# Key norms folded into the new values, token-side key scaling on ScalarE, and products of a head pair grouped by shape

## The chip, the cores and the metric

The kernel runs on one core of one Trainium2 chip. The metric is the device time of one execution in microseconds (us). Five engines work side by side, each with its own in-order instruction stream: TensorE (PE, its weight loads PEld), VectorE (DVE), ScalarE (ACT), GpSimd (POOL) and the queue that issues transfers (SP).

## The reference, cut to what matters

Two blocks follow each other on one sequence of 512 tokens with model width 1024. The first mixes a gated delta rule of 8 heads with causal attention of 8 heads and ends in a gated feed-forward; the second holds a state-space mixer (SSD) of 16 heads and a short convolution. What the change touches:

```
# gated delta rule, chunks of c tokens (the kernel: 4 chunks of 128), one head
k = l2norm(k);  q = l2norm(q) * dk**-0.5
decay = tril(exp(g_i - g_j))
lmat  = (beta*k) k^T * decay                       # the kernel's ln, with sign
sol   = solve(I + strict_lower(lmat), [beta*v, beta*k*exp(g)])
v_new = u - w @ state                              # the kernel's gvn
o     = (q*exp(g)) @ state + (q k^T * decay) @ v_new   # q k^T * decay: at
state = state*exp(g_last) + (k*exp(g_last - g))^T @ v_new   # k*exp(..): ktok

# state-space mixer, chunks of 128 tokens, heads in pairs m = 0..7
y_diag = (C B^T * decay_in) @ xd
y_off  = (C * decay_out) @ previous_state
y      = y_diag + y_off
```

## The kernel before, in words

The sequence lies along the free dimension: a tile is 128 features by 512 tokens. All weights come as one stream of 512 KB chunks (eight blocks of 128x128). ScalarE rounds a chunk into `hi`, VectorE or GpSimd makes the rest `lo`, and `linear` multiplies each block three times (hi by hi, hi by lo, lo by hi), so one linear of eight blocks is 24 products of 512 columns. These land in PSUM tiles called `mm`; all smaller products and transposes land in tiles called `pt`, of which there are four.

The order of the linears in the first block is written out by hand in `GDN_ORDER`: `kq` (key and query of a head), `vg` (value and gate), `brb` and `bra` (gates of the two branches), `low` (not a linear: it starts the norms of the attention's low-rank inputs, `cq` and `ckv`), `att` (a head of attention), `wv` (the attention's values), `ya` (output product of the delta rule). The same list orders the weight stream. Around the linears run generator tasks. A planner (`Timeline`, `drive`) prices every instruction as it is emitted and always goes on with the task whose next step is ready first by its model; the main task with the linears comes last among equals. So the instruction order of every engine is fixed when the program is built, and comes from modelled times, not from the chip's.

A head of the delta rule has two tasks. `t_gdn_a` transposes key and query to token-major, takes their squared norms on ScalarE (`ss`), turns them into reciprocal roots `r` in twelve small VectorE steps (`rsqrt`), scales the token-major key into `ktok`, and makes the two 128x128-per-chunk matrices `ln` (key by key) and `at` (key by query). At most two such tasks are open. When four heads are through, `t_solve` inverts the 32x32 diagonal blocks for these four on VectorE and GpSimd, and `t_gdn_b` (at most three open) completes the inverse and runs the four chunks of the recurrence: `gr`, `gvn` (the new values), the state `gst`, and the output. `ya` waits for all eight heads.

In the second block `t_ssd` handles a pair of heads. For each chunk it issues two products of 128 rows by 64 columns (one for each head, in the two halves of the output's partitions) and, from the second chunk on, two of 64 by 64 that add the contribution of the state before. Each fp32 product shows as two records in the trace. The loop before the change reads:

```python
for c in range(NC):
    for e in range(2):
        self.MM(py[o(e), cc], self.xd[m][:, ...], Es[e][:, cc], start=True, stop=(c == 0))
    if c:
        for e in range(2):
            self.MM(py[o(e), cc], self.st[c - 1][r, hh(e)], Cs[e][r, cc], start=False, stop=True)
```

Of the kernel before, what the change touches and what calls it, by code (L numbers as in the profile page):

```python
# [12 lines left out]
AF = mybir.ActivationFunctionType  # L13
ALU = mybir.AluOpType
# [7 lines left out]
NC = 4  # L22
# [6 lines left out]

START = ["ab", ("cq", 0), ("cq", 1), ("cq", 2)]  # L30
FIRST = [("k", 0), ("q", 0), ("k", 1)]
GDN_ORDER = [("brb", 0), ("kq", 3), ("brb", 1), ("brb", 2), ("kq", 4), ("brb", 3), ("vg", 0), ("brb", 4), ("vg",
             1), ("vg", 2), ("kq", 5), ("kq", 6), ("kq", 7), ("vg", 3), ("vg", 4), ("brb", 5), ("brb", 6),
             ("brb", 7), ("vg", 5), ("vg", 6), ("low",), ("bra", 0), ("bra", 1), ("bra", 2), ("vg", 7), ("att",
             0), ("bra", 3), ("wv", 0), ("att", 1), ("bra", 4), ("bra", 5), ("bra", 6), ("bra", 7), ("ya", 0),
             ("att", 2), ("ya", 1), ("att", 3), ("wv", 1), ("ya", 2), ("att", 4), ("ya", 3), ("att", 5), ("ya",
             4), ("att", 6), ("att", 7), ("ya", 5), ("ya", 6), ("ya", 7)]
PAIR_FFN = 3
FOLD_FFN = 3
# [360 lines left out]
class Emit:  # L400
# [564 lines left out]
    def t_gdn_a(self, h, kq):  # L965
        nc = self.nc
        hs = slice(4 * h, 4 * h + 4)
        yield self.flag("gates")

        yield lambda: "k" in kq  # L970
        k = kq["k"]
        yield [k]
        ss = self.s(8, "ss")
        pk = self.transpose4(k)
        junk = self.g(name="junk")
        yield [pk]
        for c in range(NC):
            nc.scalar.activation(junk[:, self.cc(c)], pk[:, self.cc(c)], AF.Square, accum_out=ss[:, c:c + 1])
        yield lambda: "q" in kq
        q = kq["q"]  # L980
        yield [q]
        pq = self.transpose4(q)
        yield [pq]
        for c in range(NC):
            nc.scalar.activation(junk[:, self.cc(c)], pq[:, self.cc(c)], AF.Square, accum_out=ss[:, 4 + c:5 + c])
        yield [ss]
        nc.vector.tensor_scalar(ss, ss, EPS, None, ALU.add)
        r = yield from self.rsqrt(ss, 8, "rkq")
        col = self.s(8, "kcol")
        nc.vector.tensor_tensor(col[:, 0:4], self.kdec[:, hs], r[:, 0:4], ALU.mult)  # L990
        del junk
        kt = self.g(name="ktok")
        nc.vector.tensor_tensor(self.v4(kt), self.v4(pk), self.colbc(col[:, 0:4]), ALU.mult)
        nc.vector.tensor_copy(self.rq[:, hs], r[:, 4:8])
        nc.vector.tensor_tensor(self.nk[:, hs], ss[:, 0:4], r[:, 0:4], ALU.mult)
        nc.vector.tensor_tensor(self.bk[:, hs], self.cmp[:, 64 + 4 * h:68 + 4 * h], r[:, 0:4], ALU.mult)
        nc.vector.scalar_tensor_tensor(col[:, 4:8], self.bk[:, hs], -1.0, r[:, 0:4], ALU.mult, ALU.mult)
        yield lambda: h in self.E
        e = self.E.pop(h)
        egb = self.rowload(self.grow[1, h])  # L1000
        yield [e]
        at = self.g(name="at")
        ln = self.g(name="ln")
        for t, x, f in ((ln, k, col[:, 4:8]), (at, q, r[:, 0:4])):
            p = self.mm4(k, x)
            yield [p]
            for c in range(NC):
                nc.vector.scalar_tensor_tensor(t[:, self.cc(c)], p[:, self.cc(c)], f[:, c:c + 1], e[:, self.cc(c)],
                                               ALU.mult, ALU.mult)
        yield [ln]  # L1010
        for b in range(4):
            nc.sync.dma_start(
                self.ldram[h, :, b].rearrange("c j i -> j c i"),
                self.v4(ln)[32 * b:32 * b + 32, :, 32 * b:32 * b + 32])
        yield [egb]
        nc.gpsimd.tensor_tensor(q, q, egb, ALU.mult)
        self.hd[h] = dict(kd=kt, kT=k, ln=ln, at=at, qd=q)
        self.flags.add(("L", h))
        h0 = h - h % NSOLVE
        if all(("L", i) in self.flags for i in range(h0, h0 + NSOLVE)):  # L1020
            self.spawn(self.t_solve(h0, NSOLVE), "solve")
# [29 lines left out]
    def t_gdn_b(self, h, vg):  # L1051
        nc = self.nc
# [3 lines left out]
        hs = slice(4 * h, 4 * h + 4)  # L1056
# [5 lines left out]
        ln = d.pop("ln")  # L1062
# [12 lines left out]
        p = self.transpose4(v)  # L1075
# [14 lines left out]
        p = self.pt()  # L1090
# [37 lines left out]
        for c in range(NC):  # L1128
            cc = self.cc(c)
            col = slice(4 * h + c, 4 * h + c + 1)  # L1130
            if c == 0:
                r = vb[:, cc]
            else:
                yield [st]
                p = self.pt()
                self.MM(p[:, 0:128], d["kT"][:, cc], st, start=True, stop=True)
                r = self.s(128, "gr")
                yield [p]
                nc.vector.scalar_tensor_tensor(r, p[:, 0:128], self.neg_eg[:, col], vb[:, cc],
                                               ALU.mult, ALU.add)  # L1140
            yield [Y, r]
            p = self.pt()
            self.MM(p[:, 0:128], Y[:, cc], r, start=True, stop=True)
            vn = self.s(128, "gvn")
            yield [p]
            nc.vector.tensor_scalar(vn, p[:, 0:128], self.bk[:, col], None, ALU.mult)
            yield [vn]
            if c < NC - 1:
                p = self.pt()
                self.MM(p[:, 0:128], d["kd"][:, cc], vn, start=True, stop=True)  # L1150
                st2 = self.s(128, "gst", bufs=6)
                yield [p]
                if c == 0:
                    nc.vector.tensor_copy(st2, p[:, 0:128])
                else:
                    nc.vector.scalar_tensor_tensor(st2, st, self.glast[:, col], p[:, 0:128],
                                                   ALU.mult, ALU.add)
            p = self.pt()
            if c:
                self.MM(p[:, 0:128], d["qd"][:, cc], st, start=True, stop=False)  # L1160
            self.MM(p[:, 0:128], d["at"][:, cc], vn, start=(c == 0), stop=True)
            yield [p]
            nc.scalar.copy(on[:, cc], p[:, 0:128])
            nc.scalar.activation(junk[:, cc], p[:, 0:128], AF.Square, accum_out=so[:, c:c + 1])
            if c < NC - 1:
                st = st2
# [630 lines left out]
    def t_ssd(self, m, zd):  # L1797
        nc = self.nc
        g = m // 4
        r = slice(64 * g, 64 * g + 64)  # L1800
        yield self.flag("states")
        Es, Cs = [], []
        for h in (2 * m, 2 * m + 1):
            Es.append(self.rowload(self.crow[0, h]))
            Ce = self.g(name="Ce")
            nc.sync.dma_start(Ce[r], self.crow[1, h].partition_broadcast(64))
            Cs.append(Ce)
        for e in range(2):
            h, E = 2 * m + e, Es[e]
            yield [E]  # L1810
            for c in range(NC):
                nc.vector.tensor_scalar(E[:, self.cc(c)], E[:, self.cc(c)],
                                        self.cmp2[:, 4 * h + c:4 * h + c + 1], 0.0, ALU.subtract, ALU.min)
        for e in range(2):
            yield [Es[e]]
            nc.scalar.activation(Es[e], Es[e], AF.Exp)
        for e in range(2):
            yield [Es[e]]
            nc.vector.tensor_tensor(Es[e], Es[e], self.cb[g], ALU.mult)
            yield [Cs[e]]  # L1820
            nc.gpsimd.tensor_tensor(Cs[e][r], Cs[e][r], self.C[r], ALU.mult)
        yield Es + Cs + self.st
        py = self.pt()
        o = lambda e: slice(64 * e, 64 * e + 64)
        hh = lambda e: slice(64 * ((2 * m + e) % 8), 64 * ((2 * m + e) % 8) + 64)
        for c in range(NC):
            cc = self.cc(c)
            for e in range(2):
                self.MM(py[o(e), cc], self.xd[m][:, 128 * c + 64 * e:128 * c + 64 * e + 64], Es[e][:, cc],
                        start=True, stop=(c == 0))  # L1830
            if c:
                for e in range(2):
                    self.MM(py[o(e), cc], self.st[c - 1][r, hh(e)], Cs[e][r, cc], start=False, stop=True)
        y = self.xs[m]
        yield [py]
        nc.vector.scalar_tensor_tensor(y, y, self.par("d_skip_2", m), py, ALU.mult, ALU.add)
        yield lambda: m in zd
        yield [y, zd[m]]
        nc.gpsimd.tensor_tensor(y, y, zd[m], ALU.mult)
        self.yz[g][m % 4] = y  # L1840
# [215 lines left out]
```

## Time and profile before

| | |
|---|---|
| median of 3 runs | 1463.79 us (1463.4 to 1465.91) |
| the profiled execution | 1465.11 us, span 1463.3 us |
| mean granted clock of TensorE | 0.994 |
| busy: PE / PEld / DVE / ACT / POOL | 1443.4 / 1187.8 / 867.9 / 656.2 / 497.5 us |

The span runs from the first instruction to the last; the execution's time is 1.8 us longer than its span. Busy times are sums over the span. A matmul's end is modelled, so a TensorE that counts as busy may still lose time inside its records.

### The profile page before, as it was taken

The page shows a single profiled execution, that of the slowest core. Times are in us where ns is not written, and L with a number is a line of the kernel's source. Part 1 is how long each engine was busy: PE and PEld are TensorE (multiplying, and loading weights), DVE is VectorE, ACT ScalarE, POOL GpSimd, SP SyncE. Part 2 cuts the span into 40 slices and gives each one's busy share as a digit, 9 for nine tenths or more (in the row PEclk, how much of TensorE's full clock was granted, in tenths as well). Part 3 has the DMA queues.
Part 4 walks back from the last instruction along what each step waited for, and adds up shares of the span by engine and source line. Part 5 has one row for each costly group of instructions (what it writes and reads, how often), then busy time and mean ns, then how long its engine had stood idle before and what let it go on. Part 6 is the DMA issues. An engine that isn't in the chain of part 4 may idle for free.

```text
span 1463.3 us, 18957 instructions
## 1 busy us (share of the span) xinstructions
PE 1443.4 (99%) x7084; PEld 1187.8 (81%) x7084; DVE 867.9 (59%) x1722; ACT 656.2 (45%) x1120; POOL 497.5 (34%) x312
## 2 busy tenths in 40 slices
PE   9999999999999999999999999999999999999998
PEld 6788788878878888888888888888787788788877
DVE  7988879697755555368441144347764785351164
ACT  4665336244546664354442244444544454342252
POOL 0333500520333413403554455530215444534300
PEclk9999999999999999999999999999999999999999
DMA  5434313331132224433333333232224533323333
GB/s 191 133 117 140 113 58 86 108 109 32 52 93 65 80 72 132 149 94 101 101 101 96 92 101 101 86 101 87 88 87 108 149 104 115 115 87 95 97 96 101
DMA packets 56891, 147.62 MB, mean 101 GB/s; under 512 B 15008, under 2 KB 15584, under 8 KB 56800
## 3 DMA queue, kind: packets, MB, share of 16 engines
q1 hardware_dynamic: 56800, 146.42, 33.3%
q8 instruction: 55, 0.90, 0.2%
q14 instruction: 36, 0.29, 0.1%
HBM read 139.48 MB, written 5.34 MB: 99 GB/s over the span
## 4 chain that ended last, share of the span: by engine, by line
PE 81%; DVE 11%; POOL 3%; issue 2%; ACT 1%; DMA 1%; SPq 1%; DVEq 0%; POOLq 0%; ACTq 0%
PE mm L249 72%; PE pt L249 8%; DVE lo L249 2%; POOL st L249 1%; POOL sx L249 1%; DVE st L249 1%; SPq L249 1%; DVE row L249 1%; DVE sx L249 1%; ACT hi L249 0%; DVE Y L249 0%; DVE qrs L249 0%; DMA sl<-ldram 0%; DVE v L249 0%; DMA x<-xT 0%
## 5 line engine op out<-in xcount | busy, mean ns | idle before, releaser
L249 PE MATMUL mm<-hi,hi 128*128 128x512 f32 (+2 forms) x1872 | 740.4, 395 | 1.2 <-ACT hi L249 1.2
L249 PE MATMUL mm<-hi,lo 128*128 128x512 f32 (+2 forms) x1872 | 725.4, 388 | 2.4 <-DVE lo L249 2.4
L249 PE MATMUL mm<-lo,hi 128*128 128x512 f32 (+2 forms) x1872 | 725.9, 388 | 0.8 <-DVE lo L249 0.8
L249 POOL TENSOR_TENSOR lo<-raw,hi 128x1024 fp32r<-128x1024 f32 x136 | 327.6, 2409 | 462.2 <-ACT hi L249 399.6
L249 PEld LDWEIGHTS mm<-hi,lo 128*128 128x128 f32 x1872 | 352.0, 188 | 77.2 <-DVE lo L249 3.7
L249 PEld LDWEIGHTS mm<-hi,hi 128*128 128x128 f32 x1872 | 352.4, 188 | 71.1 <-ACT hi L249 2.1
L249 PEld LDWEIGHTS mm<-lo,hi 128*128 128x128 f32 x1872 | 352.7, 188 | 67.0 <-DVE lo L249 1.5
L249 ACT ACTIVATE hi<-raw 128x1024 fp32r<-128x1024 f32 (+1 forms) x230 | 242.4, 1054 | 226.5 <-PE mm L249 168.0
L249 DVE TENSOR_TENSOR lo<-raw,hi 128x1024 fp32r<-128x1024 f32 (+1 forms) x94 | 117.1, 1245 | 27.9 <-ACT hi L249 27.9
L249 DVE TENSOR_TENSOR sq<-sq,sq 128x512 f32<-128x512 f32 x43 | 31.9, 754 | 87.9 <-ACT sq L249 87.7
L249 DVE TENSOR_TENSOR xr<-xr,mm 128x512 f32<-128x512 f32 x24 | 16.5, 687 | 86.8 <-PE mm L249 86.8
L249 DVE TENSOR_TENSOR lo<-fu,hi 128x512 fp32r<-128x512 f32 x22 | 43.1, 1960 | 40.9 <-ACT hi L249 40.9
L249 DVE SCALAR_TENSOR_TENSOR fu<-mm,params,fu 128x510 f32<-128x510 f32 (+1 forms) x38 | 28.5, 749 | 65.3 <-ACT fu L249 64.6
L249 ACT ACT_TABLE_LOAD x39 | 50.0, 1283 | 15.5 <-DVE k L249 6.0
L249 POOL TENSOR_TENSOR fu<-fg,fu 128x512 f32<-128x512 f32 x22 | 30.2, 1373 | 65.6 <-DVE fu L249 35.2
L249 POOL TENSOR_TENSOR q<-q,row 128x512 f32<-128x512 f32 x8 | 10.5, 1318 | 96.6 <-PE pt L249 86.8
L249 POOL TENSOR_TENSOR st<-sl,sx 64x247 f32<-64x247 f32 (+15 forms) x31 | 20.8, 672 | 34.3 <-DVE sx L249 25.0
L249 DVE SCALAR_TENSOR_TENSOR fg<-mm,params,fg 128x510 f32<-128x510 f32 (+1 forms) x38 | 28.2, 743 | 6.2 <-ACT fg L249 5.5
L249 DVE TENSOR_TENSOR lo<-scz,hi 128x512 fp32r<-128x512 f32 x8 | 16.2, 2020 | 26.3 <-ACT hi L249 26.3
L249 DVE TENSOR_TENSOR lo<-pt,hi 128x512 fp32r<-128x512 f32 (+3 forms) x32 | 15.6, 488 | 26.2 <-ACT hi L249 26.0
L249 ACT ACTIVATE fg<-fg 128x512 f32<-128x512 f32 x22 | 13.9, 630 | 37.0 <-DVE fg L249 37.0
L249 DVE SCALAR_TENSOR_TENSOR xbc<-mm,params,xbc 128x509 f32<-128x509 f32 (+2 forms) x30 | 22.5, 749 | 9.5 <-ACT xbc L249 8.8
(311 smaller groups left out, 1531.6 us busy)
## 6 DMA issues: line engine op xcount, KB each, us to landing
raw<-wstream SPq DMA_DIRECT2D x228, 512.0 KB, 3.6
row<-grow_d SPq DMA_DIRECT2D x16, 256.0 KB, 4.4
row<-crow_d SPq DMA_DIRECT2D x16, 256.0 KB, 5.0
x<-xT SPq DMA_DIRECT2D x8, 256.0 KB, 6.0
sbd<-gate SPq DMA_DIRECT2D x8, 256.0 KB, 2.1
sb<-sbd SPq DMA_DIRECT2D x8, 256.0 KB, 3.8
xr<-xT SPq DMA_DIRECT2D x8, 256.0 KB, 3.7
Ce<-crow_d SPq DMA_DIRECT2D x16, 128.0 KB, 5.3
```

What stands on the lines that cost most here:

```text
L249: return f(*args, **kw)
```

## The change

In the delta rule the reciprocal key norm `r` no longer enters `ktok`, `at` and the new values once each; it enters the new values alone, as its square. `ktok` is scaled by the decay factor only, which is known before the norms, by four ScalarE copies right behind the key's squares; `at` is one VectorE product for all four chunks in place of four. The small column tiles change with it. In `t_ssd` all eight 128x64 products of a pair are issued first and then all six 64x64 products, with the accumulation flags to match. `GDN_ORDER` is a new list.

```diff
-GDN_ORDER = [("brb", 0), ("kq", 3), ("brb", 1), ("brb", 2), ("kq", 4), ("brb", 3), ("vg", 0), ("brb", 4), ("vg",
-             1), ("vg", 2), ("kq", 5), ("kq", 6), ("kq", 7), ("vg", 3), ("vg", 4), ("brb", 5), ("brb", 6),
-             ("brb", 7), ("vg", 5), ("vg", 6), ("low",), ("bra", 0), ("bra", 1), ("bra", 2), ("vg", 7), ("att",
-             0), ("bra", 3), ("wv", 0), ("att", 1), ("bra", 4), ("bra", 5), ("bra", 6), ("bra", 7), ("ya", 0),
-             ("att", 2), ("ya", 1), ("att", 3), ("wv", 1), ("ya", 2), ("att", 4), ("ya", 3), ("att", 5), ("ya",
+GDN_ORDER = [("kq", 3), ("brb", 0), ("brb", 1), ("brb", 2), ("kq", 4), ("vg", 0), ("brb", 3), ("brb", 4), ("vg",
+             1), ("vg", 2), ("kq", 5), ("kq", 6), ("kq", 7), ("vg", 3), ("vg", 4), ("brb", 5), ("vg", 5), ("brb",
+             6), ("brb", 7), ("bra", 0), ("bra", 1), ("vg", 6), ("low",), ("bra", 2), ("vg", 7), ("bra", 3),
+             ("att", 0), ("bra", 4), ("bra", 5), ("wv", 0), ("att", 1), ("bra", 6), ("bra", 7), ("ya", 0),
+             ("att", 2), ("ya", 1), ("att", 3), ("ya", 2), ("att", 4), ("wv", 1), ("att", 5), ("ya", 3), ("ya",
              4), ("att", 6), ("att", 7), ("ya", 5), ("ya", 6), ("ya", 7)]
@@ t_gdn_a, behind the squares of the key
+        kt = self.g(name="ktok")
+        for c in range(NC):
+            nc.scalar.activation(kt[:, self.cc(c)], pk[:, self.cc(c)], AF.Copy,
+                                 scale=self.kdec[:, 4 * h + c:4 * h + c + 1])
+        del pk
@@ t_gdn_a, behind the reciprocal roots
-        col = self.s(8, "kcol")
-        nc.vector.tensor_tensor(col[:, 0:4], self.kdec[:, hs], r[:, 0:4], ALU.mult)
+        col = self.s(4, "kcol")
-        kt = self.g(name="ktok")
-        nc.vector.tensor_tensor(self.v4(kt), self.v4(pk), self.colbc(col[:, 0:4]), ALU.mult)
-        nc.vector.tensor_tensor(self.bk[:, hs], self.cmp[:, 64 + 4 * h:68 + 4 * h], r[:, 0:4], ALU.mult)
-        nc.vector.scalar_tensor_tensor(col[:, 4:8], self.bk[:, hs], -1.0, r[:, 0:4], ALU.mult, ALU.mult)
+        nc.vector.tensor_tensor(col, self.cmp[:, 64 + 4 * h:68 + 4 * h], r[:, 0:4], ALU.mult)
+        nc.vector.scalar_tensor_tensor(self.bk[:, hs], col, -1.0, r[:, 0:4], ALU.mult, ALU.mult)
@@ t_gdn_a, ln and at
-        for t, x, f in ((ln, k, col[:, 4:8]), (at, q, r[:, 0:4])):
-            p = self.mm4(k, x)
-            yield [p]
-            for c in range(NC):
-                nc.vector.scalar_tensor_tensor(t[:, self.cc(c)], p[:, self.cc(c)], f[:, c:c + 1], e[:, self.cc(c)],
-                                               ALU.mult, ALU.mult)
+        p = self.mm4(k, k)
+        yield [p]
+        for c in range(NC):
+            nc.vector.scalar_tensor_tensor(ln[:, self.cc(c)], p[:, self.cc(c)], self.bk[:, 4 * h + c:4 * h + c + 1],
+                                           e[:, self.cc(c)], ALU.mult, ALU.mult)
+        p = self.mm4(k, q)
+        yield [p]
+        nc.vector.tensor_tensor(at, p, e, ALU.mult)
@@ t_gdn_b
-            nc.vector.tensor_scalar(vn, p[:, 0:128], self.bk[:, col], None, ALU.mult)
+            nc.vector.tensor_scalar(vn, p[:, 0:128], self.bk[:, col], -1.0, ALU.mult, ALU.mult)
@@ t_ssd
-                        start=True, stop=(c == 0))
-            if c:
-                for e in range(2):
-                    self.MM(py[o(e), cc], self.st[c - 1][r, hh(e)], Cs[e][r, cc], start=False, stop=True)
+                        start=(c == 0), stop=False)
+        for c in range(1, NC):
+            cc = self.cc(c)
+            for e in range(2):
+                self.MM(py[o(e), cc], self.st[c - 1][r, hh(e)], Cs[e][r, cc], start=False,
+                        stop=(c == NC - 1))
```

## Rows read from the trace of the kernel before

**Rows 1.** The page: busy time by engine, and shares of the chain that ended last.

```profile
PE 1443.4 (99%) x7084; PEld 1187.8 (81%) x7084; DVE 867.9 (59%) x1722; ACT 656.2 (45%) x1120; POOL 497.5 (34%) x312
...
PE 81%; DVE 11%; POOL 3%; issue 2%; ACT 1%; DMA 1%; SPq 1%; DVEq 0%; POOLq 0%; ACTq 0%
```

**Rows 2.** Windows: stretch, length, busy PE, PEld, DVE, ACT, POOL, clock, DMA.

```profile
160.00:190.00 30.00, 28.27 (x196) 22.81 (x195) 22.84 (x53) 10.99 (x23) 9.90 (x12) 0.94 0.36 104
...
205.00:260.00 55.00, 54.62 (x301) 45.57 (x300) 52.49 (x171) 29.82 (x81) 3.60 (x4) 1.00 0.30 86
...
310.00:340.00 30.00, 27.54 (x196) 23.17 (x195) 22.50 (x65) 9.79 (x28) 2.78 (x2) 0.83 0.31 87
...
360.00:420.00 60.00, 57.23 (x309) 47.48 (x309) 49.07 (x116) 30.49 (x68) 19.69 (x11) 0.98 0.26 79
...
1123.00:1285.00 162.00, 161.73 (x851) 127.35 (x852) 96.68 (x144) 74.49 (x93) 75.63 (x42) 1.00 0.39 114
1285.00:1403.00 118.00, 118.00 (x526) 97.72 (x525) 30.73 (x43) 39.96 (x52) 41.41 (x18) 1.00 0.35 103
```

**Rows 3.** Chain that ended last, 1055 to 1300 us: start, length, what.

```profile
1074.56 5.46 PE mm L249 x24
...
1106.87 1.51 PE pt L249 x16
...
1123.27 4.91 PE pt L249 x54
...
1147.29 2.42 PE pt L249 x28
```

**Rows 4.** Timeline of TensorE across one head pair: start, length, records of one shape.

```profile
1147.22 0.66 PE L249 MATMUL pt<-row,xd 128*64 128x128 f32 x8
1147.80 0.44 PE L249 MATMUL pt<-Ce,st 64*64 64x128 f32 x4
1148.17 0.44 PE L249 MATMUL pt<-row,xd 128*64 128x128 f32 x4
...
1149.27 0.44 PE L249 MATMUL pt<-Ce,st 64*64 64x128 f32 x4
1149.64 0.50 PE L249 MATMUL mm<-hi,hi 128*128 128x512 f32 x1
```

**Rows 5.** Timeline of the weight loads in the same pair, idle before in brackets.

```profile
1147.80 0.19 PEld L249 LDWEIGHTS pt<-Ce,st 64*64 64x64 f32 x4 [0.17 <-issue]
```

**Rows 6.** Timeline of VectorE in the first head's t_gdn_a.

```profile
75.08 0.16 DVE L249 TENSOR_TENSOR kcol<-kdec,rkq 128x4 f32<-128x4 f32 x1
75.28 0.69 DVE L249 TENSOR_TENSOR ktok<-pt,kcol 128x512 f32<-128x512 f32 x1
75.89 0.16 DVE L249 COPY rq<-rkq 128x4 f32<-128x4 f32 x1
...
82.58 1.12 DVE L249 SCALAR_TENSOR_TENSOR at<-pt,rkq,row 128x128 f32<-128x128 f32 x4
```

**Rows 7.** Groups by shape: VectorE's scaling of a PSUM tile by a broadcast.

```profile
L249 DVE TENSOR_TENSOR xd<-pt,dt 128x512 f32<-128x512 f32 x8 | 5.5, 692 | 8.0 <-PE pt L249 8.0
```

**Rows 8.** Groups by shape: ScalarE's 128x128 copies.

```profile
L249 ACT COPY X<-pt 128x128 f32<-128x128 f32 x32 | 8.5, 265 | 37.5 <-PE pt L249 31.2 <-issue 5.9
...
L249 ACT ACTIVATE P<-P,su 128x128 f32<-128x128 f32 x8 | 3.2, 397 | 1.6 <-DVE su L249 1.4
```

**Rows 9.** Timeline of TensorE at its longest wait in the first block.

```profile
325.62 0.79 PE L249 MATMUL pt<-T,yodd 64*64 64x64 f32 x5 [2.15 <-DVE T L249]
```

**Rows 10.** Windows of 5 us behind that wait, columns as in the second group.

```profile
330.00:335.00 5.00, 5.00 (x25) 4.59 (x23) 1.71 (x10) 0.53 (x3) 0.00 (x0) 0.50 0.01 2
```

**Rows 11.** Low-rank norms, by tile: lengths in ns, first and last start.

```profile
L249 ACT ACTIVATE sq<-lr x5: 612/615/632, 309.9 to 313.4; 128x512 f32<-128x512 f32 x5
...
L249 DVE TENSOR_TENSOR lo<-lr,hi x5: 682/685/686, 356.2 to 362.8; 128x512 fp32r<-128x512 f32 x5
```

**Rows 12.** Windows of the linears' tile alone: busy PE, PEld, DVE, ACT.

```profile
310.00:347.00 37.00, 15.15 (x49) 8.78 (x47) 0.00 (x0) 1.18 (x2) 0.86 0.25 70
```

## The prediction

> **What bounds the kernel now.** I read the page's busy line and its chain first, then the windows, then the chain of the second block, and last the timelines. The page says TensorE: 1443.4 us busy of a 1463.3 us span, and 81% of the chain [rows 1]. The reader is to see next that this has two meanings. From 1123 to 1403 us TensorE is full but for 0.3 us at the very start of the stretch [rows 2], so time taken out of its work there is time off the end, as long as the weights keep up. In the first block it is also nearly always busy, but three stretches lose time in two ways: they stand idle for 1.73, 2.46 and 2.77 us (length minus busy, 160 to 190, 310 to 340, 360 to 420), and their clock is granted only in part, 0.94, 0.83 and 0.98 [rows 2]. Taking the granted share as full work done, that is another 1.8, 5.1 and 1.2 us. Together the three lose 15 us, half of it (7.6) in 310 to 340. There a recurrence product waits 2.15 us for a VectorE result [rows 9], and behind the wait a stretch that is full by its records runs at a granted 0.50, the lower level of 1.2 GHz [rows 10]. VectorE, not the linears, sets the pace of these stretches; between them, in 205 to 260, VectorE is busy 52.49 of 55 us while TensorE idles 0.38 [rows 2].
>
> **The head pairs' products.** One pair is a single piece of the chain, 28 records in 2.42 us, and two pairs that stand together are 54 records (two of 56 are missing) in 4.91 [rows 3]; there are eight pairs. The timeline shows why a pair takes that long. The eight records of one shape at its head last 0.58 us from start to start, each later group of four 0.37 (1147.80 to 1148.17; the last, 1149.27 to 1149.64, alike) [rows 4]. So four more records of one shape cost 0.58 - 0.37 = 0.21, and a change of shape costs 0.37 - 0.21 = 0.16; the weight loads stand idle for 0.17 ahead of the first load of the new shape [rows 5], which is the same gap seen from the other side. Before, the 28 records are seven fours in six runs of one shape (the first run has two fours): 6 x 0.16 + 7 x 0.21 = 2.43, as measured. After, there are two runs: 16 records of 128x64 in 0.37 + 3 x 0.21 = 1.00, and 12 of 64x64 in 0.37 + 2 x 0.21 = 0.79, together 1.79. That saves 0.63 a pair, **5.0 us** over eight. Bounds: that a long 64x64 run keeps the pace is not shown, since before it never has more than four records; if each four of them still took 0.37, the pair would take 1.00 + 1.11 = 2.11 and the saving be 2.5. The nearest row for a slow run, 16 records in 1.51 us (states, 128x64) [rows 3], is for products that stay in one half of the output's partitions for eight records on end; the pairs alternate between the halves, before and after, so I take 5.0. The upper end is 5.0 too, because the number of products and loads is unchanged. Everything the products read is waited for ahead of the first one, so no wait moves.
>
> **The key's token-side scaling.** VectorE loses one `kcol` product (0.20 to the next start) and `ktok` (0.61 to the next start) [rows 6]; `at` falls from 1.12 for four pieces [rows 6] to one 128x512 product out of PSUM, 0.69 by the nearest such row [rows 7]. The other small steps keep their number, and `gvn` gains a second constant factor in an instruction that is there already; I cost that at nothing, with nothing to cover it if it isn't. That is 0.20 + 0.61 + 0.43 = 1.24 us a head, 9.9 us of VectorE in all. ScalarE gains four 128x128 copies a head: 265 ns each as a plain copy, 397 with a column as scale [rows 8], so 1.1 to 1.6 us a head, 9 to 13 in all. They stand in ScalarE's queue behind the key's squares; behind them wait the weight rounding and the convolutions' first taps. ScalarE is busy 29.8 of 55 us in the tightest stretch [rows 2], so I cost them at nothing; without that cover they would delay a weight chunk by up to 1.6 us eight times. The key's PSUM tile comes free before the norms; with TensorE full at that time this is worth nothing by itself.
>
> The Trainium skill speaks against this move: its page "ScalarE: Activation LUTs", section "Rules for kernel authors", wants plain multiplications on VectorE, not on ScalarE. By its costs four such copies are, as an estimate, 1.2 us for 0.7 of VectorE. The rows agree on the prices; as ScalarE has the room and VectorE has not, the sum stays the same by either.
>
> What VectorE's 9.9 us are worth to TensorE: nothing from 205 to 310, where linears fill it. They let the second group of four heads start its inverse some 3 x 1.24 = 3.7 us sooner, and count only where TensorE waits, so at most the 15 us above.
>
> **The new order.** Key and query of head 3 come one linear earlier, 5.46 us [rows 3], so the first inverse may start that much sooner. Value and gate of head 6 come two linears later, behind `bra` 0 and 1; then head 6 no longer runs its recurrence in step with heads 4 and 5 at 310 to 340, where 7.6 us are lost, and its linears fill that place. `low` moves behind head 6, out of the same place, with its squares, sums and roots on ScalarE and VectorE. No transfer is added; the weight stream only follows the list. What this gives can't be read exactly, since the planner lays all instructions out anew, in the second block too. Bounds: 15 us gained if all losses go; 7.6 us lost for each new stall like the one at 325. I take **3.5**, a little under half of the loss at 310 to 340, and nothing elsewhere.
>
> **Sum.** 5.0 + 3.5 = 8.5 us. Against the profiled execution's own 1465.11 that is 1456.6; it ran 1.3 us above the median of the runs, 1463.79, against which the forecast is 1455.3. I round to 1456, since the whole gain of the order is soft.
>
> **Rivals.**
> - *Only the products gain.* The new layout finds as many stalls as the old: 1463.8 - 5.0 = 1458.8. For it: the planner doesn't see the real waits, as the 2.15 us one shows. Against it: VectorE has 9.9 us less to do.
> - *Most of the first block's losses go.* 10 of the 15 us: 1463.8 - 5.0 - 10 = 1448.8. For it: shorter stalls also keep the clock at its full level, which doubles their worth. Against it: the waits lie on chains of VectorE steps that the change leaves alone.
> - *One more stall with a slow clock behind it*, in head 6's or 7's recurrence, which now runs with less beside it: 1463.8 - 5.0 + 7.6 = 1466.4, about no change.
> - *Attention waits for its norms* (the other side). From `low` to the last rounded input took 309.9 to 363.5 us [rows 11], with linears and recurrence in between all along. After, only `bra` 2, `vg` 7 and `bra` 3 stand between `low` and the first attention head: 4 x 5.46 = 21.8 us of linears. At 310 to 347 the linears had 15.15 of 37 us [rows 12], and at that rate 21.8 last 53 us, just as long as the norms took. If the recurrences fill less, the main task stands still; half of the 32 us that could be uncovered, 16, gives 1463.8 - 5.0 + 16 = 1475. It decides from 8 us on (5.0 and 0.2%). Against it: the norms took that long because VectorE was crowded at 310 to 340.
> - *The grouping doesn't speed up the products*, because the gap belongs to the two accumulating products on one place and not to the shape: then only the order's 3.5 remain, 1460.3. Against it: the weight loads stand idle too [rows 5], at every change alike.
>
> **How the numbers follow.** 0.2% (2.9 us) is about what a measurement of this kernel can tell from no change. Chances: the forecast 0.40, only the products 0.22, most losses gone 0.14, one more stall 0.12, attention waits 0.06, no faster products 0.06. The range 1448 to 1466 takes in all but the last rival on the slow side, half of the best case and a part of the added stall, about 0.16 outside. Faster (under 1460.9): 0.38 + 0.20 + 0.14 + 0.03 = 0.75; slower (over 1466.7): 0.06 + 0.04 = 0.10; the rest, 0.15, within 0.2%.
>
> **What would show it.** Each pair as 28 records of TensorE in 1.8 us with one change of shape inside; VectorE's sum near 858 us with no `ktok`, ScalarE's near 667 with 32 short copies; TensorE full from the pairs to 1395; the idle time and clock in the stretch of heads 4 to 6 better than 2.46 us and 0.83. The prediction is wrong if a pair still takes 2.1 us or more, if weight chunks come late in the second block, or if a new idle place with a lower clock behind it appears around the first attention head.

## The result and the profile after

The changed kernel takes 1452.56 us, the median of 4 runs (1451.21 to 1453.24), against 1463.6 for the kernel before in the same comparison (4 runs, 1462.92 to 1465.91). The ratio is 0.9919, with a 95% interval of 0.9907 to 0.9931: 11 us faster, where 7.6 had been forecast. The profiled execution took 1452.72 us (span 1450.9) at a mean granted clock of 0.999.

The page of the kernel after, busy time by engine and the shares of the chain, answering to [rows 1]:

```profile
PE 1435.9 (99%) x7084; PEld 1183.8 (82%) x7084; DVE 864.1 (60%) x1717; ACT 665.4 (46%) x1152; POOL 470.3 (32%) x277
...
PE 87%; DVE 9%; DMA 2%; issue 1%; ACT 1%; SPq 0%; POOL 0%; DVEq 0%; ACTq 0%; POOLq 0%
```

TensorE has the same 7084 records, is busy 7.5 us less, and holds 87% of the chain instead of 81%. So it both has less to do and waits less. The windows of the kernel after tell the two apart; columns as in [rows 2], and the last row answers to its last:

```profile
160.00:190.00 30.00, 27.89 (x198) 21.84 (x198) 24.59 (x64) 10.64 (x21) 5.31 (x6) 1.00 0.34 89
...
205.00:260.00 55.00, 55.00 (x304) 46.25 (x302) 50.30 (x151) 32.87 (x97) 5.39 (x6) 1.00 0.33 93
...
310.00:340.00 30.00, 30.00 (x202) 25.39 (x202) 17.71 (x60) 14.58 (x41) 5.22 (x3) 1.00 0.19 56
...
360.00:420.00 60.00, 59.55 (x329) 49.62 (x329) 42.54 (x113) 33.08 (x73) 17.21 (x10) 1.00 0.24 71
...
1280.00:1395.00 115.00, 115.00 (x513) 95.20 (x512) 30.04 (x42) 40.65 (x54) 39.02 (x17) 1.00 0.33 101
```

From 310 to 340 TensorE is full and its clock fully granted, where it lost 7.6 us before; 160 to 190 is idle for 2.11 us, but keeps its clock. From the pairs on TensorE is as full as before.

Where the 12.4 us of span went is read from landmarks: pieces of the chain that have the same length and number of records in both kernels. First the chain of the kernel before, then that of the kernel after (start, length, what):

```profile
555.01 85.41 PE mm L249 x378
...
1291.50 101.37 PE mm L249 x447
...
1418.05 41.19 PE mm L249 x203
```

```profile
546.90 85.41 PE mm L249 x378
...
1115.19 3.96 PE pt L249 x54
...
1137.56 1.83 PE pt L249 x28
...
1278.90 101.37 PE mm L249 x447
...
1405.46 41.20 PE mm L249 x203
```

The long stretch of linears behind the first block begins 8.1 us sooner, and the first two pairs, at 1115.19 for 1123.27 [rows 3], still 8.1. Behind the last pair it is 12.6. So in these two executions **the first block gave 8.1 us and the pairs 4.5**: 0.95 for the two that stand together (4.91 to 3.96), 0.59 for each of the six others (2.42 to 1.83 for five of them; one stands in a piece with four records more).

The inside of a pair, first on TensorE and then in the weight loads of the kernel after, answers to [rows 4, 5]:

```profile
1137.49 1.09 PE L249 MATMUL pt<-row,xd 128*64 128x128 f32 x16
1138.51 0.87 PE L249 MATMUL pt<-Ce,st 64*64 64x128 f32 x12
1139.31 0.50 PE L249 MATMUL mm<-hi,hi 128*128 128x512 f32 x1
```

```profile
1138.51 0.63 PEld L249 LDWEIGHTS pt<-Ce,st 64*64 64x64 f32 x12 [0.17 <-issue]
```

Two groups in 1.02 and 0.80 us from start to start, and the gap of 0.17 before the loads stands once inside the pair.

Groups by shape of the kernel after (busy us, mean ns of one; then the idle time ahead), VectorE's `at` and `lo` and ScalarE's `ktok`:

```profile
L249 DVE TENSOR_TENSOR lo<-raw,hi 128x1024 fp32r<-128x1024 f32 x95 | 120.8, 1272 | 26.7 <-ACT hi L249 26.6
...
L249 DVE TENSOR_TENSOR at<-pt,row 128x512 f32<-128x512 f32 x8 | 5.5, 682 | 0.8 <-PE pt L249 0.8
...
L249 ACT ACTIVATE ktok<-pt,kdec 128x128 f32<-128x128 f32 x32 | 9.3, 398 | 0.0
```

and `lo` in the kernel before, where VectorE split three weight chunks fewer (GpSimd three more):

```profile
L249 DVE TENSOR_TENSOR lo<-raw,hi 128x1024 fp32r<-128x1024 f32 x92 | 115.7, 1257 | 27.9 <-ACT hi L249 27.9
```

### The profile page after: what moved, and what is told of

Its sections match the earlier page's. It is cut to its first block, busy times and chain, and to the rows that moved or that the text cites. A ratio compares the mean times of both kernels' runs of the same rounds, so it can differ in the third digit from the quotient of the medians.

```text
span 1450.9 us, 18951 instructions
## 1 busy us (share of the span) xinstructions
PE 1435.9 (99%) x7084; PEld 1183.8 (82%) x7084; DVE 864.1 (60%) x1717; ACT 665.4 (46%) x1152; POOL 470.3 (32%) x277
## 4 chain that ended last, share of the span: by engine, by line
PE 87%; DVE 9%; DMA 2%; issue 1%; ACT 1%; SPq 0%; POOL 0%; DVEq 0%; ACTq 0%; POOLq 0%
PE mm L249 78%; PE pt L249 9%; DVE lo L249 2%; DVE st L249 1%; DVE v L249 1%; DMA raw<-wstream 1%; DMA sl<-ldram 1%; DVE sx L249 1%; DVE rq_u L249 0%; SPq L249 0%; ACT hi L249 0%; DVE Y L249 0%; DVE row L249 0%; DVE x L249 0%; DVE sq L249 0%
## 5 line engine op out<-in xcount | busy, mean ns | idle before, releaser
L249 PE MATMUL mm<-hi,hi 128*128 128x512 f32 (+1 forms) x1872 | 742.5, 397 | 0.7 <-ACT hi L249 0.7
L249 PE MATMUL mm<-hi,lo 128*128 128x512 f32 (+1 forms) x1872 | 725.3, 388 | 1.9 <-DVE lo L249 1.9
L249 PE MATMUL mm<-lo,hi 128*128 128x512 f32 (+1 forms) x1872 | 726.0, 388 | 0.8 <-DVE lo L249 0.8
L249 POOL TENSOR_TENSOR lo<-raw,hi 128x1024 fp32r<-128x1024 f32 x133 | 321.1, 2415 | 490.8 <-ACT hi L249 460.4
L249 ACT ACTIVATE hi<-raw 128x1024 fp32r<-128x1024 f32 (+1 forms) x230 | 242.6, 1055 | 246.2 <-PE mm L249 168.6
L249 DVE TENSOR_TENSOR lo<-raw,hi 128x1024 fp32r<-128x1024 f32 (+1 forms) x97 | 122.1, 1260 | 26.7 <-ACT hi L249 26.6
L249 DVE SCALAR_TENSOR_TENSOR fg<-mm,params,fg 128x510 f32<-128x510 f32 (+1 forms) x38 | 28.3, 744 | 6.2 <-ACT fg L249 5.5
L249 ACT COPY X<-pt 128x128 f32<-128x128 f32 x32 | 8.5, 265 | 47.1 <-PE pt L249 37.7
```

What stands on the lines that cost most here:

```text
L249: return f(*args, **kw)
```

## The experiments

Each comparison is against runs of the kernel before on the same chip, and the intervals are of 95%. To read the first block in each trace I take three things. Its end is the start of the 85.41 us stretch shown above. "Idle" is length minus busy PE in a window. "Loss" is idle plus the ungranted share of the clock, summed over windows of 20 us up to that end; it is 21.6 us in the kernel before and 9.5 in the kernel after. One execution's first block can move by some us, so where there are timed runs they decide. The granted clock is shown to two decimals, so a loss is good to about one us.

**The pairs alone.** The kernel before with the new loop in `t_ssd` and nothing else.

```diff
-                        start=True, stop=(c == 0))
-            if c:
-                for e in range(2):
...
+                        start=(c == 0), stop=False)
+        for c in range(1, NC):
+            cc = self.cc(c)
+            for e in range(2):
```

> The kernel before with the regrouped head pairs alone. If a change of shape costs what the trace of before showed, each pair is some 0.6 us shorter and the time falls by 4.5 to 5 us; the first block, up to the first long stretch of the feed-forward's linears, ends where it did. If the saving needs the new layout of the first block, the time falls by under 2 us.

Measured 1459.42 us (12 runs), ratio 0.9969 (0.9957 to 0.9982). Single pairs take 1.83, and the first block ends at 556.4 us, for 555.0 before. From the first block's end to the end of the span it takes 904.1 us, against 908.3 before; in every kernel of this study but the one of the head-by-head products it is 903.8 to 904.1 with the new loop and 908.3 to 908.7 without it. The pairs are worth 4.4 us, whatever the first block does.

**The order alone, the norms alone, both.** The kernel before with the new `GDN_ORDER`; with the new lines of `t_gdn_a` and `t_gdn_b`; and the kernel after with the old loop in `t_ssd`.

```diff
-GDN_ORDER = [("brb", 0), ("kq", 3), ("brb", 1), ("brb", 2), ("kq", 4), ("brb", 3), ("vg", 0), ("brb", 4), ("vg",
+GDN_ORDER = [("kq", 3), ("brb", 0), ("brb", 1), ("brb", 2), ("kq", 4), ("vg", 0), ("brb", 3), ("brb", 4), ("vg",
...
```

> The kernel before with the new order list alone; pairs and norms as before. Theory: the order took the stall with the slow clock out of the first block, so this gives 6 to 8 us. Rival: VectorE's shorter key steps did it, and the order alone gives under 2 us. A third: the order was made for the new steps and costs time with the old ones (slower by 1 us or more).

> The kernel before with the new norms and the key scaling on ScalarE alone; order list and pairs as before. Theory of the order: 0 to 2 us, the stall at 325 us stays. Rival, VectorE's relief of 1.24 us a head: 6 to 8 us, and the stall is gone with the old order too.

> Norms, key scaling and order, with the head pairs as before: the complement of the pairs alone. If the parts add up, 11.0 less the pairs' 4.5 is left, 6.5 us in the runs' medians; in the trace the first block ends 8 us earlier, as in the changed kernel. If it ends otherwise, the planner's new layout moves with each part and the sum isn't one of parts.

Measured, all against the same runs of the kernel before: order alone 1470.97 us (7 runs), ratio 1.0038 (1.0025 to 1.0051), slower; norms alone 1465.53 (11 runs), 1.0004 (0.9992 to 1.0016), the same; both 1456.44 (5 runs), 0.9945 (0.9931 to 0.9959). Against that comparison's 1464.86 the parts give +6.1 and +0.7, and together -8.4: **15 us of the first block (14 by the ratios) belong to neither part, but to their meeting**. A sum over parts, as the prediction made it, can't show that. With the pairs there is no such meeting: 0.9945 and 0.9969 multiply to 0.9914, and the kernel after measured 0.9919. Each single part was laid out in one way only; that it is worth nothing in any layout is not shown.

**The key's scaling back on VectorE.** The kernel after with one VectorE product at the same place.

```diff
-        for c in range(NC):
-            nc.scalar.activation(kt[:, self.cc(c)], pk[:, self.cc(c)], AF.Copy,
-                                 scale=self.kdec[:, 4 * h + c:4 * h + c + 1])
+        nc.vector.tensor_tensor(self.v4(kt), self.v4(pk), self.colbc(self.kdec[:, hs]), ALU.mult)
```

> The changed kernel, but the key tokens are scaled by one VectorE product (128x512, 0.69 us) at the place of the four ScalarE copies. If the move of this work to ScalarE brings the time, VectorE has 5.5 us more to do in the first block and the kernel is 2 to 4 us slower than the changed one (1455 to 1457). If ScalarE was the wrong engine for it, 0 to 2 us faster. If neither is at its limit there, within 1.5 us, apart from what a new layout by the planner does.

Measured 1467.61 us (10 runs, 1461.61 to 1473.61), ratio 1.0015 (0.9995 to 1.0035): no better than before, though the pairs' 4.4 us are in it. So about 14 us (0.9919 against 1.0015) hang on eight instructions of 0.69 us, 5.5 in all. Windows of this kernel, from an execution of 1472.67 us:

```profile
205.00:260.00 55.00, 49.98 (x264) 42.02 (x263) 44.00 (x140) 27.32 (x81) 3.27 (x3) 0.97 0.25 70
```

TensorE is idle for 5 us here, where it had no idle time with the copies on ScalarE. The product's own group, first in this kernel, then in the kernel before (busy us, mean ns; then VectorE's idle time ahead):

```profile
L249 DVE TENSOR_TENSOR ktok<-pt,kdec 128x512 f32<-128x512 f32 x8 | 5.5, 689 | 6.6 <-ACT junk L249 6.5
```

```profile
L249 DVE TENSOR_TENSOR ktok<-pt,kcol 128x512 f32<-128x512 f32 x8 | 5.5, 691 | 0.3
```

At this place VectorE stands still for 6.6 us ahead of the product, nearly all of it until ScalarE's squares of the key (`junk`) are through, which read the same PSUM tile; in the kernel before, behind the roots, it stood still for 0.3. So the run doesn't price 5.5 us of work on VectorE alone. What can't be told apart is how much of the 14 us is VectorE's own time, how much these waits, and how much the other instruction order that the planner then lays out; a product on VectorE behind the roots, with the new order, was not tried.

**Half of the new order.** The list's front (up to `vg` 4) and its tail changed separately, the rest as in the kernel after: new front with old tail, then old front with new tail. The first, against the kernel after:

```diff
-             1), ("vg", 2), ("kq", 5), ("kq", 6), ("kq", 7), ("vg", 3), ("vg", 4), ("brb", 5), ("vg", 5), ("brb",
-             6), ("brb", 7), ("bra", 0), ("bra", 1), ("vg", 6), ("low",), ("bra", 2), ("vg", 7), ("bra", 3),
...
+             1), ("vg", 2), ("kq", 5), ("kq", 6), ("kq", 7), ("vg", 3), ("vg", 4), ("brb", 5), ("brb", 6),
+             ("brb", 7), ("vg", 5), ("vg", 6), ("low",), ("bra", 0), ("bra", 1), ("bra", 2), ("vg", 7), ("att",
...
```

> The changed kernel with the first half of the new list (up to vg 4) and the second half of the old one. Theory: the new tail, with head 6 and low later, keeps the recurrences of heads 4 to 6 out of step; without it the first block ends at 554 us or later instead of 547, and the clock falls again between 310 and 340. Rival: head 3 earlier is what counts; then this ends at 547 to 549.

> The changed kernel with the old first half of the list and the new second half (head 6 and low later). Theory of the tail: the first block ends at 547 to 549 us, no fall of the clock between 310 and 340. Rival, head 3 earlier: 554 or later. A third: both halves are needed, since any other layout meets a stall somewhere; then this and the run with the new front both end at 552 or later.

> The same kernel as the run with the old front and the new tail, whose single execution had every product of TensorE take more than twice as long, from the first to the last. If that belongs to the execution, this one runs at the usual pace and tells of the tail: first block ending at 547 to 549 us if the tail is what counts, at 552 or later if both halves are needed. If it belongs to the kernel, 3138 us again.

New front with old tail: 1468.23 us, one run, longer than any of the 13 runs of the kernel before beside it (1461.69 to 1467.5). Old front with new tail: a first execution took 3138.02 us (last section); repeated, 1462.33 (8 runs), ratio 0.9983 (0.9973 to 0.9993), less than the pairs alone give. Neither half does it. VectorE's timeline shows why: the product `vb` opens a head's recurrence. First the kernel before, then the kernel after, then the new front with the old tail (start, length, tile, how many together):

```profile
312.51 1.88 DVE L249 TENSOR_TENSOR vb<-pt,nk 128x512 f32<-128x512 f32 x3
```

```profile
302.18 0.68 DVE L249 TENSOR_TENSOR vb<-pt,nk 128x512 f32<-128x512 f32 x1
302.85 0.68 DVE L249 TENSOR_TENSOR vb<-pt,nk 128x512 f32<-128x512 f32 x1
...
336.74 0.68 DVE L249 TENSOR_TENSOR vb<-pt,nk 128x512 f32<-128x512 f32 x1
```

```profile
300.29 1.29 DVE L249 TENSOR_TENSOR vb<-pt,nk 128x512 f32<-128x512 f32 x2
...
331.65 0.68 DVE L249 TENSOR_TENSOR vb<-pt,nk 128x512 f32<-128x512 f32 x1
```

Before, heads 4, 5 and 6 start their recurrence together at 312.5. After, 4 and 5 start ten us sooner and 6 at 336.7. The early start goes back to the inverse of the second four heads (`t_solve`). Half of its instructions, by engine, the transfer that brings its input and the one that takes its result out, first before, then after (count, shortest/median/longest in ns, first and last start):

```profile
L249 DVE TENSOR_TENSOR st<-sl,sx x16: 215/321/1283, 268.1 to 305.4; 64x112 f32<-64x112 f32 x2, 64x135 f32<-64x135 f32 x2, 64x156 f32<-64x156 f32 x2, 64x175 f32<-64x175 f32 x2
L249 POOL TENSOR_TENSOR st<-sl,sx x15: 235/616/1678, 275.6 to 308.5; 64x240 f32<-64x240 f32 x2, 64x247 f32<-64x247 f32 x2, 64x252 f32<-64x252 f32 x2, 64x255 f32<-64x255 f32 x2
L249 SPq DMA_DIRECT2D sl<-ldram x1: 473/473/473, 262.9 to 262.9; - x1
L249 SPq DMA_DIRECT2D xdram<-sx x1: 456/456/456, 309.1 to 309.1; - x1
```

```profile
L249 DVE TENSOR_TENSOR st<-sl,sx x24: 182/354/2309, 261.1 to 294.3; 64x112 f32<-64x112 f32 x2, 64x135 f32<-64x135 f32 x2, 64x156 f32<-64x156 f32 x2, 64x175 f32<-64x175 f32 x2
L249 POOL TENSOR_TENSOR st<-sl,sx x7: 232/589/1467, 280.2 to 296.6; 64x255 f32<-64x255 f32 x1, 64x252 f32<-64x252 f32 x1, 64x247 f32<-64x247 f32 x1, 64x240 f32<-64x240 f32 x1
L249 SPq DMA_DIRECT2D sl<-ldram x1: 473/473/473, 256.4 to 256.4; - x1
L249 SPq DMA_DIRECT2D xdram<-sx x1: 457/457/457, 297.2 to 297.2; - x1
```

The input is fetched 6.5 us sooner, and from there to the result it takes 40.8 us instead of 46.2. The planner now gives VectorE 24 of the 31 steps instead of 16; that this is what shortens it is not shown, since with 4 of 31 there the norms alone take 44.9. In every kernel of this study with the new front and the key's copies on ScalarE the result goes out between 293.6 and 299.3 us, in every other at 305.3 or later: order alone 310.4, norms alone 310.7, old front with new tail 305.3, and 319.3 with the product back on VectorE. So the front makes the early start together with the norms, and as early with the old tail; what is missing there is work for TensorE beside it. Windows of the linears' tile alone, of the same three kernels in the same order (columns as in [rows 12]):

```profile
310.00:340.00 30.00, 11.55 (x38) 7.00 (x37) 0.00 (x0) 1.18 (x2) 0.83 0.31 87
```

```profile
310.00:340.00 30.00, 22.77 (x78) 13.26 (x78) 2.24 (x3) 2.48 (x4) 1.00 0.19 56
```

```profile
310.00:340.00 30.00, 15.75 (x44) 8.77 (x45) 2.25 (x3) 0.69 (x1) 0.81 0.13 36
```

The new tail puts `bra` 0 and 1 ahead of `vg` 6, so that 22.8 us of linears lie beside the two recurrences instead of 11.6 or 15.8. With the old tail TensorE runs dry at 302 us. Its timeline there, in the kernel with the new front and the old tail:

```profile
302.71 0.65 PE L249 MATMUL pt<-X,T 128*64 128x64 f32 x8 [0.87 <-DMA X<-xdram]
305.22 1.11 PE L249 MATMUL pt<-T,yodd 64*64 64x64 f32 x8 [1.87 <-DVE T L249]
```

and windows behind these waits, where the clock is at its lower level as in [rows 10], so that 2.7 us of waits are followed by another 5 lost (0.50 of 10 us). Not every wait is followed so: behind one of 2.76 us at 318 us the kernel with the order alone has 0.66 from 318 to 323 and 1.00 from there. What decides is not shown. The windows:

```profile
311.00:316.00 5.00, 5.00 (x26) 3.92 (x25) 3.28 (x7) 0.37 (x1) 0.00 (x0) 0.50 0.19 36
316.00:321.00 5.00, 5.00 (x16) 4.32 (x17) 1.33 (x4) 0.53 (x3) 0.00 (x0) 0.50 0.18 72
```

The idle time of TensorE by stretch, worked out from such windows (granted clock behind it where under 1.00), with the end of the first block and its loss. Each row is one execution: that of the order alone was the fastest of its seven (1467.70 us, median 1470.97), that of the norms alone the slowest of its eleven (1469.93, median 1465.53).

| kernel | 160-190 | 190-260 | 260-310 | 310-340 | 360-420 | end | loss |
|---|---|---|---|---|---|---|---|
| before | 1.73 (.94) | .38 | .22 | 2.46 (.83) | 2.77 (.98) | 555.0 | 21.6 |
| order alone | 1.87 (.94) | 1.11 | 2.73 | 2.85 (.94) | 1.85 | 557.3 | 19.2 |
| norms alone | 1.48 (.97) | 2.67 (.92) | 3.90 (.98) | .80 (.98) | .21 | 559.9 | 23.6 |
| new front, old tail | 2.00 | .09 | 3.48 (.94) | .63 (.81) | 2.67 (.97) | 562.6 | 28.3 |
| old front, new tail | .73 | 3.15 (.98) | 3.55 | .00 (.94) | 2.33 | 556.7 | 19.7 |
| norms and order | 2.02 | .09 | .21 | .09 | .43 | 547.3 | 9.0 |
| after | 2.11 | .09 | .48 | .00 | .45 | 546.9 | 9.5 |

Each partial kernel only moves the hole: with the order alone, the norms alone or the old front and new tail the second inverse is still late, and TensorE waits ahead of the recurrences behind it (190 to 310); with the new front and the old tail it waits within them. Only where the early inverse meets the linears laid beside it are both holes shut, and all eight heads are through by 402 us (the last `ga`) instead of 418.6 before and 412 to 425 in the partial kernels.

**Is it the luck of one layout?** The kernel after with one number of the planner changed, which lays all instructions out anew.

```diff
-LAT = {"DVE": 33, "ACT": 33, "PE": 53, "POOL": 78, "SP": 60}
+LAT = {"DVE": 33, "ACT": 35, "PE": 53, "POOL": 78, "SP": 60}
```

> The changed kernel with one number of the planner's model changed (ScalarE's latency 33 to 35 ns): the same instructions, laid out a little differently from the first block on. If the gain belongs to the new steps and list as such, the first block ends at 546 to 549 us. If it is the luck of one layout, it ends anywhere from 547 to 560, as the three earlier kernels with the other combinations did (555 to 560).

> The version that ended its first block earliest so far (the changed kernel with the planner's ScalarE latency at 35 ns), now timed. From its one look, 1449 us against 1452.6 of the changed kernel. If the layout is what gives it, 1448 to 1450 and a ratio to the kernel before near 0.990; if that look was a lucky execution, 1452 to 1453.

One execution took 1448.96 us, and the same kernel on another chip 1452.15 (4 runs, 1450.62 to 1452.62), ratio 0.991 (0.9894 to 0.9927). So the low first time was that execution's or that chip's; the new layout keeps the gain. The first block ended at 543.4 and 546.5 in the two profiles of this one kernel: differences of 3 us in that column mean nothing. The two kernels of the next experiment were laid out anew as well: the steps and list of the kernel before end their first block at 553.3 us there (555.0 before), those of the kernel after at 548.6 (546.9).

**What the pairs' price belongs to.** The kernel before (with the planner's number changed as above) with the seven groups of a pair so ordered that there are still six runs of one shape, but no product stands right behind the one that it adds to; and the kernel after (`"DVE": 35` in the same list) with two runs, but all products of one head ahead of the other's, so that the halves of the output's partitions no longer alternate. In the first diff x is 1 for a group of 128x64, and c is its chunk.

```diff
-        for c in range(NC):
+        for n, (x, c) in enumerate(((1, 2), (1, 1), (0, 2), (1, 3), (0, 1), (1, 0), (0, 3))):
```

```diff
-        for c in range(NC):
-            cc = self.cc(c)
-            for e in range(2):
+        for e in range(2):
+            for c in range(NC):
+                cc = self.cc(c)
```

> The kernel before, with two edits far apart. The products of a head pair keep six runs of one shape, but no product follows the one that it adds to (chunks 2, 1 of the 128x64 products, then 2 of the 64x64, and so on). If a change of shape is what costs, a pair takes 2.42 us as before; if the accumulation on one place is, about 1.8 us. And the planner's ScalarE latency is 35 in place of 33 ns, to see what another layout does to the old steps and list: the first block of before ends at 555 us; if the old version is as sensitive to its layout as the new one, this ends 4 us or more away from it on either side.

> The changed kernel, with two edits far apart. A pair's products go head by head: eight records in one half of the output's partitions, then eight in the other, then six and six, still two runs of one shape. If alternating between the halves lets two products run side by side, a pair takes longer by about 28 x 0.04 = 1.1 us (0.094 us a record, as the states' products showed, in place of 0.053), near 2.9; if the halves don't matter, 1.8 as in the changed kernel. And the planner's VectorE latency is 35 in place of 33 ns: if new steps and list keep the gain in any layout, the first block ends at 543 to 549 us; if not, 555 or later.

A pair in the chain, first with six runs and no neighbouring sums, then with two runs head by head:

```profile
1145.58 2.42 PE pt L249 x28
```

```profile
1140.04 2.58 PE pt L249 x28
```

Six runs cost 2.42 as before (1463.81 us in all, one run), with the new accumulation flags too: the gap belongs to the change of shape, and neither to the sums on one place nor to the flags. Head by head costs 2.58 (2.9 had been expected), 0.75 more than 1.83, and gives back more than the grouping brought: from the first block's end to the end of the span it takes 909.3 us (1459.69 in all, one run). The alternation between the halves has to stay inside the run.

## Why the prediction was right, point by point

- **The pairs: right in mechanism, a little large.** 5.0 us forecast, 4.4 to 4.5 measured. A pair takes 1.83, not 1.79: 1.02 and 0.80 for the two runs against 1.00 and 0.79. The rest of the difference is the two pairs that stand together, which gave 0.95 and not 1.26. The lower bound, that a long 64x64 run is slow, did not hold: 12 records take 0.80. The rival that blamed the sums on one place is refuted by the six runs kept apart. The Trainium skill, page "TensorEngine Tiling (Array Packing)", section "Key Properties", says that a change of the tiling mode drains TensorE and that different tiles work in parallel. The trace agrees with both and adds the prices in this kernel: 0.15 us a change (0.59 over the four that went), and 0.75 a pair when the two halves no longer alternate.
- **VectorE's relief and ScalarE's load: sizes right, worth misjudged.** `at` fell from 9.0 us in the sum to 5.5 and `ktok`'s 5.5 left VectorE, as reckoned; ScalarE grew by 9.2 (9 to 13 expected). VectorE's total is 864 and not near 858: the planner gave it three more weight chunks to split, 5.1 us, and 16 more steps of the two inverses (32 instructions), which GpSimd had before. Costing the move at nothing by itself was right: the norms alone measure 0.04% slower, within the noise. But inside the new order it decides: it belongs to the early second inverse, which the prediction reckoned 3.7 us sooner and then gave no price. With the product back on VectorE, at the copies' place, the gain is gone. The Trainium skill's advice to keep plain multiplications on VectorE (page "ScalarE: Activation LUTs", section "Rules for kernel authors") would have cost at that place: a ratio of 1.0015 against 0.9919, the waits for the squares included.
- **The order: the step that was mis-sized, and credited wrongly.** The prediction said 3.5 us, "a little under half of the loss at 310 to 340, and nothing elsewhere". The first block gave 8.1 us in the two profiles, about 6.6 in the medians (11.0 less 4.4), and 8.4 in the kernel with norms and order and the old pairs. Its picture was right: head 6 falls out of step, linears fill its place, and 310 to 340 loses nothing any more. But it stopped at that stretch, while 360 to 420 lost 2.77 us before and loses 0.45 now, at a clock of 1.00. And it held the order to be the cause: alone the order costs 6 us. So the total came out near with a term that was too small and stood for the wrong cause; that part was luck.
- **Where the first block's gain stayed short of its losses.** The loss fell by 12.1 us (21.6 to 9.5), the first block by 8.1. TensorE's records at full clock take some 4 us more (537.4 against 533.4). The new layout changes between shapes more often: counted record by record up to that end, TensorE goes 57 times instead of 45 from one of 128x128, 128x64 and 64x64 to another. At the pairs' 0.15 us, an estimate, that is 1.8 us; the rest stays open.
- **The rivals.** "Most of the first block's losses go" (1448.8) was the nearest of them: the result lies halfway between it and the forecast. "One more stall with a slow clock" didn't come about in this kernel, but with the new front and the old tail it did, with just that pattern. "Attention waits for its norms" did not: TensorE is full at 310 to 340 and idle for 0.18 us from 340 to 360 and 0.45 from 360 to 420.

## What to carry to other kernels

In a program whose order is laid out in advance, an earlier result and a new order of the filling work can each be worth nothing or less and yet gain together: build all four combinations before one is thrown away, and read the idle time by stretch to see whether a hole was shut or only moved. Moving a small step from one engine to another is judged by what it waits for in that engine's order and by when its result is waited for, not by its duration alone. Small products of several shapes go together by shape, but within a shape neighbours should keep alternating between the halves of the output's partitions.

## What the runs showed of the hardware that was not expected

One execution of the old front with the new tail took 3138.02 us, where the same kernel took 1462.33 in 8 runs afterwards on another chip; the other kernels on the first chip kept the usual pace. Its windows far from any wait, and then a stretch of the repeat:

```profile
2000.00:2100.00 100.00, 100.00 (x216) 63.65 (x215) 23.79 (x24) 20.26 (x26) 27.66 (x14) 1.00 0.15 47
```

```profile
1200.00:1240.00 40.00, 40.00 (x197) 32.83 (x196) 21.85 (x32) 18.79 (x23) 21.98 (x12) 1.00 0.40 116
```

TensorE starts 216 records in 100 us, 0.463 each, where a linear's 24 take 5.46 [rows 3], 0.228 each: about half the pace, from the first block to the end, while VectorE's splitting of a weight chunk took its usual time (1245 and 1285 ns). The columns say a clock of 1.00, but the page has no row of granted clocks for that execution, so that the clock stood at its lower level throughout would fit and is not shown. A mean granted clock can mislead on a smaller scale too: one run of the kernel with ScalarE's 35 in the planner is listed at 0.949 and took 1452.14 us, as long as two of its neighbours at 0.998 and 0.999. The execution of 3138.02 us enters no comparison here.
